# Eight of the mixer's sixteen gate tiles taken out of the recurrence and computed in pairs by seven block products

## The chip, the core and the metric

The kernel runs on one core of one Trainium2 chip. The metric is the device time of one launch in microseconds (us). Five engines work side by side: TensorE (PE in the rows; PEld is its weight load), VectorE (DVE), ScalarE (ACT), GpSimd (POOL) and SyncE (SP), whose queue issues all the transfers spoken of here. Each engine takes its instructions in a fixed order; where one waits, those behind it wait too.

## The reference, cut to what matters

One decoder block over a sequence of 1024 tokens, width 1024: a SwiGLU sublayer, a token mixer, a second SwiGLU sublayer. The change touches two factors of the mixer, the gates g_pool and g_dn, each a product of the normed input with 1024 columns of one weight:

```
proj = h @ mix_w_in
xp, q, k, v, z, b_raw, a_raw, g_pool, g_dn = split(proj)
ya = multiscale_pool(xp) @ pool_w * pool_scale @ pool_proj
o  = gated_delta_rule(q, k, v, ...)          # the recurrence
yb = (rms_norm(o) * silu(z)) @ dn_proj
merged = sigmoid(g_pool) * ya + sigmoid(g_dn) * yb
return merged @ mix_w_out
```

## The kernel before

**Number format.** Every large product is made in three parts: a float32 operand is split into a rounded high part (a cast on ACT, line 134) and the rest (a subtraction on DVE, line 135), and `mm3` (line 165) adds high x high, high x low and low x high. A product of a 128-wide weight tile with one half of the sequence (512 columns) over all 1024 inputs is so 8 x 3 = 24 matmuls of 128x512; a tile of 128 outputs for both halves is 48.

**Stages.** `ffn1`, then the mixer, then `mout` (merge and output projection), then `ffn2`. Both FFN stages use Strassen-Winograd block products (`both`, line 461): a 2 x 2 matrix of weight blocks times a 2 x 2 matrix of blocks of the input takes seven block products of 12 matmuls instead of eight. They need four sums of blocks of the input (`h_sums`, line 376), made once and kept, and sums of weight blocks and of results for each pair, all elementwise on 128x512 tiles.

**The mixer.** It runs 17 units, numbered here from u = 0 to 16. Unit u prepares one half-sequence of one head (`prepare`, line 1087: a chain of 15 steps that alternate between PE and ACT or DVE) and scans the half that unit u - 1 prepared (`scan`, line 1184: four chunks of three steps and an end with a norm and four transposes, line 1233). The last unit, 16, only scans. Into these chains `weave` (line 1354) hands out fill in equal shares: `z`, `q`, `k`, `v` and pool projections and the sixteen gate tiles (`gate_out`, line 1246: 48 matmuls, a sigmoid for each half, a store to `sg_dram`). Odd units 1, 3, 5 and 7 also hold one pool group. The number of gate tiles in a unit is `n`: one in each odd unit from 1 to 13, two in unit 14, four in unit 15, and the three that are left in unit 16.

**Order.** The code is written for a scheduling layer that gives instructions priority by their place in the program, assigns them to engine queues when their inputs are ready by its own model, and reuses memory of a closed pool tile by tile. What it made of the code is a fixed list for each engine.

**After the mixer.** `reload` (line 745) brings back twelve tiles per half (four pooled `p_dram`, eight `y_dram`) through the old x tiles and splits them; `merge` (line 761) multiplies them by the output projections in `ps_t` and `ps_pj` and by the gates read from `sg_dram`. Sums of the conditioning weights `ada_w` (line 201, DVE) run between.

Of the kernel before, what the change touches and what calls it, by code (L numbers as in the profile page):

```python
# [21 lines left out]
NH = T // HALF  # L22
NC = HALF // P
HEADS = 8
# [24 lines left out]
N_MID = 3  # L49
N_OUT = 11  # L50
GROUP = 4
END_PAD = 224
PSUM_OUT = ("inv", "inv", "scan", "oo")

# [12 lines left out]
def block(tc, ctx, xT, vec, cst, invw, ada_w, f1_in, f1_out, f2_in, f2_out, mix_in, mix_ba,  # L67
          pool_w, pool_proj, dn_proj, mix_out, outT):
    nc = tc.nc
# [63 lines left out]
    def split(src, hi, lo, lo_eng=V):  # L133
        S.copy(hi, src)  # L134
        lo_eng.tensor_tensor(out=lo, in0=src, in1=hi.bitcast(F32), op=ALU.subtract)  # L135

    def load(src, t=None):
        t = raw_tile(src.shape[-1]) if t is None else t
        nc.sync.dma_start(t, src)
        return t  # L140
# [205 lines left out]
        return gh, gl  # L346


    def ffn(fpool, x, h, w_in, w_out, gate, done, between=(), first=None):


# [4 lines left out]
        sums = {}  # L356
# [7 lines left out]
        def middle(f, hf, w):  # L364
# [1 line left out]
            mm3(pg, tiles(w[0], KD, h[hf]))  # L366
            mm3(pu, tiles(w[1], KD, h[hf]))
            return swiglu(pg, pu)

        def sub(out, a, b, eng=V):  # L370
            eng.tensor_tensor(out=out, in0=a, in1=b, op=ALU.subtract)  # L371

        def f32(t):
            return t.bitcast(F32)

        def h_sums():

# [67 lines left out]
            early_outs(js, 1)  # L445
            return islice(steps, N_OUT - N_MID)

        def terms(ps, a, b, c, start, stop, chained):

            for n, (u, v) in enumerate(((a[0], b[0]), (a[0], b[1]), (a[1], b[0]))):  # L450
                PE.matmul(ps, lhsT=u[:, c * P:(c + 1) * P], rhs=v, start=start and n == 0,  # L451
                          stop=stop and n == 2, skip_group_check=chained)

        def product(ps, src, hs, start=True):

            w = pair()
            split(src, *w)
            for k in range(4):
                terms(ps, w, hs[k], k, start and k == 0, k == 3, not start)

        def both(f, out, pairs=False):

            (a11, a12), (a21, a22) = [[load(w_in[f, :, i, c * HALF:(c + 1) * HALF])
                                       for c in range(2)] for i in range(2)]
            h11, h21, h22 = h[0][:4], h[0][4:], h[1][4:]
            s1, s2 = nt[:, 0, :], nt[:, 1, :]
# [10 lines left out]
            c11, c12 = bank("pj"), bank("t")  # L477
            product(c11, a11, h11)
            yield
            u = act()  # L480
            S.copy(u, c11)
            V.tensor_tensor(out=s1, in0=a21, in1=a22, op=ALU.add)
            product(c12, s1, sums["1"])
            yield
            v = act()
            S.copy(v, c12)
            sub(s2, s1, a11)
            product(c11, a12, h21, start=False)
            yield
            g0 = act()  # L490
            S.activation(g0, c11, AF.Silu)
            p6 = bank("pj")
            product(p6, s2, sums["2"])
            yield
            V.tensor_tensor(out=u, in0=u, in1=p6, op=ALU.add)
            sub(s2, a12, s2)
            product(c12, s2, h22, start=False)
            yield
            g1 = act()
            V.tensor_tensor(out=g1, in0=u, in1=c12, op=ALU.add)  # L500
            S.activation(g1, g1, AF.Silu)
            p7 = bank("t")
            sub(s1, a11, a21)
            product(p7, s1, sums["3"])
            yield
            V.tensor_tensor(out=u, in0=u, in1=p7, op=ALU.add)
            V.tensor_tensor(out=v, in0=u, in1=v, op=ALU.add)
            p4 = bank("pj")
            product(p4, a22, sums["4"])
            yield  # L510
            V.tensor_tensor(out=u, in0=u, in1=p4, op=ALU.subtract)
            gated_tile(g0, u)
            gated_tile(g1, v)

        def out_group(fs, gs):

# [219 lines left out]
    with phase_pool("mix") as rows, phase_pool("parts") as parts, phase_pool("odds") as odds:  # L736
        wring.set((wpool, 3), (rows, 5))
        mixer(tc, BySize(rows, parts, odds), locals())


    with phase_pool("ffn2") as fpool:
# [68 lines left out]
def mixer(tc, mp, env):  # L810
# [488 lines left out]


    qkv = {0: lead}
    gates = [gate_out(i, m) for m in range(KD) for i in range(2)]
    pools = [pool_group(g) for g in range(4)]
    mixes = []
    zs, preps, states, ds = {}, {}, {}, {}
# [7 lines left out]
    for u in range(HEADS * NH + 1):  # L1313
        hd, hf = divmod(u, NH)
        fill = []
        if hf == 0 and hd < HEADS:
            zs[hd] = []
            fill.append((16, gate_z(hd, zs[hd])))
        if mixes:
            fill.append((2, mixes.pop(0)))  # L1320
        if hf == 0 and hd < HEADS:
            if hd + 1 < HEADS:
                qkv[hd + 1] = [[], [], [], []]
                fill += [(16, conv(4 + j * HEADS + hd + 1, qkv[hd + 1])) for j in range(2)]
            n = 0 if hd + 1 < HEADS else 2
        elif hd + 1 < HEADS:
            fill.append((16, conv(4 + 2 * HEADS + hd + 1, qkv[hd + 1])))
            n = 1
        else:
            n = 4 if hd < HEADS else len(gates)  # L1330
        if pools and hf == 1:
            fill.append((16, pools.pop(0)))
            mixes.append(pool_mix(4 - 1 - len(pools)))
        for _ in range(min(n, len(gates))):
            fill.append((16, gates.pop(0)))
        steps = []
# [115 lines left out]
```

## Time and profile before

| what | value |
| --- | --- |
| time, median of 3 runs | 2526.25 us (2524.32 to 2527.13) |
| the profiled execution's own time | 2523.53 us |
| its span in the trace | 2521.7 us |
| PE busy in the span | 2455.1 us (97%) |
| DVE busy | 1930.0 us (77%) |
| ACT busy | 999.4 us (40%) |
| mixer, start of unit 1 to the last transposes of unit 16 | 829.0 to 1591.6 us |

Matmuls are pipelined: the next one starts before the last ends, so the busy time of PE overstates its work, and what a matmul costs is read from the distance between starts, or from a count over a stretch in which PE never pauses.

### The profile page before, as it was taken

To read this page: it belongs to the slowest core of one execution; us is meant where nothing else is said; L and a number is where in the kernel's file an instruction comes from. 1 tells how busy PE (TensorE), PEld (TensorE's weight loads), DVE (VectorE), ACT (ScalarE), POOL (GpSimd) and SP (SyncE) were. 2 spreads that over 40 slices of the span, in tenths; PEclk is the share of its full clock that TensorE was granted. 3 is DMA by queue.
4 is the path that set the end of the run, shared out by engine and by line. 5 is a ranking of instruction groups with operands and counts; after the bars stand their busy time and mean duration, and the time that the engine had idled before them with its cause. 6 is when DMAs were issued, how large, how long until landed. Compare 5 with 4: busy or idle time off the path is not lost. (4 is left out here: it accounts for less than half of the span.)

```text
span 2521.7 us, 33597 instructions
## 1 busy us (share of the span) xinstructions
PE 2455.1 (97%) x12496; PEld 2000.6 (79%) x12496; DVE 1930.0 (77%) x3300; ACT 999.4 (40%) x1689; POOL 210.9 (8%) x228
## 2 busy tenths in 40 slices
PE   7899999999999999999999999999999999999997
PEld 4678888888767888888888888788777888888875
DVE  6988888888887776867877853767687668788897
ACT  3333333333456444544544542311453233333333
POOL 0500000000030101102000000000241000000003
PEclk9999999999999999999999999999999999999998
DMA  7234322222231112121111122854221122222232
GB/s 271 80 117 137 127 71 68 67 80 80 87 131 43 55 48 73 47 66 58 51 47 42 47 85 88 273 170 159 88 76 46 49 65 84 68 71 71 68 94 77
DMA packets 121556, 222.09 MB, mean 88 GB/s; under 512 B 13616, under 2 KB 14384, under 8 KB 121392
## 3 DMA queue, kind: packets, MB, share of 16 engines
q1 hardware_dynamic: 121392, 219.95, 27.0%
q8 instruction: 98, 1.61, 0.3%
q14 instruction: 66, 0.54, 0.1%
HBM read 194.73 MB, written 25.17 MB: 87 GB/s over the span
## 5 line engine op out<-in xcount | busy, mean ns | idle before, releaser
L134 ACT CAST whi<-raw 128x512 fp32r<-128x512 f32 (+1 forms) x403 | 248.2, 618 | 606.5 <-PE ps_pj L165 155.8
L135 DVE TENSOR_TENSOR wlo<-raw,whi 128x512 fp32r<-128x512 f32 (+1 forms) x403 | 289.1, 722 | 75.3 <-ACT whi L134 73.3
L165 PE MATMUL ps_pj<-hh,whi 128*128 128x512 f32 (+1 forms) x732 | 304.5, 416 | 0.0
L165 PE MATMUL ps_pj<-hh,wlo 128*128 128x512 f32 (+1 forms) x732 | 289.7, 396 | 2.0 <-DVE wlo L135 2.0
L165 PE MATMUL ps_pj<-hl,whi 128*128 128x512 f32 (+1 forms) x732 | 289.5, 396 | 0.0
L134 ACT CAST whi<-nt 128x512 fp32r<-128x512 f32 x160 | 99.5, 622 | 263.3 <-PE ps_pj L451 125.1
L165 PEld LDWEIGHTS ps_pj<-hh,wlo 128*128 128x128 f32 (+1 forms) x732 | 137.1, 187 | 31.2 <-DVE wlo L135 2.5
L135 DVE TENSOR_TENSOR wlo<-nt,whi 128x512 fp32r<-128x512 f32 x160 | 110.1, 688 | 62.6 <-ACT whi L134 62.5
L165 PEld LDWEIGHTS ps_pj<-hh,whi 128*128 128x128 f32 (+1 forms) x732 | 137.5, 188 | 24.2 <-issue 2.9
L165 PEld LDWEIGHTS ps_pj<-hl,whi 128*128 128x128 f32 (+1 forms) x732 | 137.8, 188 | 23.1 <-issue 1.4
L451 PE MATMUL ps_pj<-hh,wlo 128*128 128x512 f32 x320 | 124.8, 390 | 1.0 <-DVE wlo L135 1.0
L451 PE MATMUL ps_pj<-hh,whi 128*128 128x512 f32 x320 | 125.1, 391 | 0.5 <-ACT whi L134 0.5
L451 PE MATMUL ps_pj<-hl,whi 128*128 128x512 f32 x320 | 124.8, 390 | 0.0
L895 DVE SCALAR_TENSOR_TENSOR cacc<-rawseq,vt,cacc 128x512 f32<-128x512 f32 x144 | 107.1, 744 | 0.6
L165 PE MATMUL ps_pj<-hxh,whi 128*128 128x512 f32 (+1 forms) x252 | 103.2, 410 | 0.0
L165 PE MATMUL ps_pj<-hxh,wlo 128*128 128x512 f32 (+1 forms) x252 | 99.0, 394 | 0.4 <-DVE wlo L135 0.4
L165 PE MATMUL ps_pj<-hxl,whi 128*128 128x512 f32 (+1 forms) x252 | 98.8, 393 | 0.0
L226 POOL TENSOR_TENSOR act<-act,nt 128x512 f32<-128x512 f32 x18 | 26.4, 1468 | 807.9 <-ACT nt L233 807.5
L567 DVE SCALAR_TENSOR_TENSOR x<-ps_inv,mod,x 128x512 f32<-128x512 f32 x128 | 89.3, 743 | 0.2
L451 PE MATMUL ps_inv<-opl,whi 128*128 128x512 f32 x224 | 87.7, 392 | 0.0
L451 PE MATMUL ps_inv<-oph,whi 128*128 128x512 f32 x224 | 87.2, 391 | 0.0
L451 PE MATMUL ps_inv<-oph,wlo 128*128 128x512 f32 x224 | 86.8, 389 | 0.0
(477 smaller groups left out, 6367.9 us busy)
## 6 DMA issues: line engine op xcount, KB each, us to landing
raw<-f_in SPq DMA_DIRECT2D x184, 256.0 KB, 3.4
raw<-f_out SPq DMA_DIRECT2D x160, 256.0 KB, 2.8
raw<-ada_w SPq DMA_DIRECT2D x112, 256.0 KB, 3.1
raw<-mix_in SPq DMA_DIRECT2D x104, 256.0 KB, 2.8
ada_raw<-ada_w SPq DMA_DIRECT2D x32, 256.0 KB, 5.3
sg_dram<-sg SPq DMA_DIRECT2D x32, 256.0 KB, 2.0
act<-sg_dram SPq DMA_DIRECT2D x32, 256.0 KB, 3.9
raw<-dn_proj SPq DMA_DIRECT2D x20, 256.0 KB, 3.0
```

The lines of the kernel that those rows point to most:

```text
L134: S.copy(hi, src)
L135: lo_eng.tensor_tensor(out=lo, in0=src, in1=hi.bitcast(F32), op=ALU.subtract)
L165: PE.matmul(ps, lhsT=a, rhs=b, start=n == 0, stop=n == last)
L226: eng.tensor_tensor(out=a, in0=a, in1=b, op=ALU.add)
L451: PE.matmul(ps, lhsT=u[:, c * P:(c + 1) * P], rhs=v, start=start and n == 0, stop=stop and n == 2, skip_group_check=chained)
L567: V.scalar_tensor_tensor(out=x[k][hf], in0=banks[m], scalar=mod[:, gate, k:k + 1], in1=x[k][hf], op0=ALU.mult, op1=ALU.add)
L895: V.scalar_tensor_tensor(out=acc, in0=raw[:, i:i + HALF], scalar=w[:, i:i + 1], in1=acc, op0=ALU.mult, op1=ALU.add)
```

## The change

The generator of the seven products moves out of the FFN into a function `seven` that the FFN and the new code share; the FFN's instructions are the same ones. Of the sixteen gate tiles eight (m = 0 to 3, for both gates) stay in the recurrence: none in units 1, 3, 5 and 7, one each in 9, 11, 13 and 14, two in 15, two in 16. The other eight (m = 4 to 7) form a new stage, `gates`, between the mixer and `mout`: for each m the 2 x 2 matrix of weight blocks has the two gates as rows and the two halves of the 1024 inputs as columns. `gate_sums` makes the four sums of input blocks first, all on DVE and ACT; then four times seven products follow.

```diff
+N_PLAIN = 4
+N_GATE_ACT = 8
...
+    def seven(blocks, h, sums, known):
+        (a11, a12), (a21, a22) = [[load(blocks(i, c)) for c in range(2)] for i in range(2)]
+        h11, h21, h22 = h[0][:4], h[0][4:], h[1][4:]
+        s1, s2 = nt[:, 0, :], nt[:, 1, :]
+        c11, c12 = bank("pj"), bank("t")
+        product(c11, a11, h11)
...
+        S.copy(u, c11)
+        V.tensor_tensor(out=s1, in0=a21, in1=a22, op=ALU.add)
+        product(c12, s1, sums["1"])
...
+        product(c11, a12, h21, start=False)
...
+        known(0, 0, c11)
+        p6 = bank("pj")
+        product(p6, s2, sums["2"])
...
+        product(c12, s2, h22, start=False)
...
+        product(p7, s1, sums["3"])
...
+        product(p4, a22, sums["4"])
+        yield
+        V.tensor_tensor(out=u, in0=u, in1=p4, op=ALU.subtract)
+        known(1, 0, u)
+        known(1, 1, v)
...
+    with phase_pool("gates") as gp:
+        aring.set((gp, N_GATE_ACT))
+        wring.set((wpool, 3))
+        sums = {n: [] for n in "1234"}
+        def gate_sums():
...
+            for k in range(4):
+                b12, t1 = added(h[1][k]), act()
+                less(t1, b12, h[0][k])
+                kept("1", t1)
+                b22 = added(h[1][k + 4])
+                sub(b12, b22, b12)
+                kept("3", b12)
+                sub(b22, b22, t1)
+                kept("2", b22)
+                less(b22, b22, h[0][k + 4])
+                kept("4", b22, h_pair(1, k))
+                yield
...
+        for _ in gate_sums():
+            pass
+        for m in range(N_PLAIN, KD):
+            for _ in gates_of(m):
+                pass
...
-    gates = [gate_out(i, m) for m in range(KD) for i in range(2)]
+    gates = [gate_out(i, m) for m in range(N_PLAIN) for i in range(2)]
...
-            n = 0 if hd + 1 < HEADS else 2
+            n = 0 if hd + 1 < HEADS else 1
...
-            n = 1
+            n = 0 if pools else 1
...
-            n = 4 if hd < HEADS else len(gates)
+            n = 2 if hd < HEADS else len(gates)
```

(`added` is one DVE addition of a high and a low part, `less` two subtractions, `sub` one, `kept` a split, which is one cast on ACT and one subtraction on DVE.)

**DVE, end of the last unit.** Before: L1223 to L1235 are the end of the last scan, L201 the `ada_w` sums, `pl` the first split of the reloaded pool tiles.

```order
L1201 TENSOR_SCALAR vn<-ps_scan,beta 128x128
L201 SCALAR_TENSOR_TENSOR nt<-raw,sc,nt 128x512 x2
L1223 TENSOR_REDUCE so<-sqd 128x4
L1224 SCALAR_TENSOR_TENSOR so<-so,qeps 128x4
L1229 TENSOR_TENSOR x_91<-ps_oo,so 128x512
L201 SCALAR_TENSOR_TENSOR nt<-raw,sc,nt 128x512 x4
L1235 SCALAR_TENSOR_TENSOR x_92<-ps_oo,vt,z 128x512
L201 SCALAR_TENSOR_TENSOR nt<-raw,sc,nt 128x512
L135 TENSOR_TENSOR pl<-x_85,ph 128x512
```

The same place after; L1288 to L1300 are the end of the scan under new line numbers, L770 and L352 the additions and subtractions of `gate_sums`, `t1l` and `t3l` its splits.

```order
L1266 TENSOR_SCALAR vn<-ps_scan,beta 128x128
L1288 TENSOR_REDUCE so<-sqd 128x4
L1289 SCALAR_TENSOR_TENSOR so<-so,qeps 128x4
L1294 TENSOR_TENSOR x_91<-ps_oo,so 128x512
L1300 SCALAR_TENSOR_TENSOR x_92<-ps_oo,vt,z 128x512
L770 TENSOR_TENSOR act<-hxh,hxl 128x512
L352 TENSOR_TENSOR act<-act,hh 128x512
L770 TENSOR_TENSOR act<-hh,hl 128x512
L352 TENSOR_TENSOR act<-act,hl 128x512
L352 TENSOR_TENSOR act<-act 128x512
L770 TENSOR_TENSOR act<-hxh,hxl 128x512
L137 TENSOR_TENSOR t1l<-act,t1h 128x512
```

The whole of `gate_sums` stands behind the last instruction of the last scan, L1300; nothing of it is ahead.

**PE, behind the last transposes** (L1233 before, L1298 after). Before, the merge's products of the reloaded pool tiles `ph` and `pl` come next:

```order
L165 MATMUL ps_pj<-hh,wlo 128x512
L1233 MATMUL ps_oo<-ct,x_91 128x128 x4
L165 MATMUL ps_t<-ph,whi 128x512
L165 MATMUL ps_t<-pl,whi 128x512
L165 MATMUL ps_t<-ph,wlo 128x512
```

After, twelve matmuls on stored input blocks (`hh`, `hl`; the last one is the first row here), then those that read the sums `t1` and `t2`:

```order
L360 MATMUL ps_pj<-hh,wlo 128x512
L360 MATMUL ps_t<-t1h,whi 128x512
L360 MATMUL ps_t<-t1l,whi 128x512
L360 MATMUL ps_t<-t1h,wlo 128x512
L360 MATMUL ps_pj<-t2h,whi 128x512
L360 MATMUL ps_pj<-t2l,whi 128x512
L360 MATMUL ps_t<-t1h,whi 128x512
L360 MATMUL ps_t<-t1l,whi 128x512
L360 MATMUL ps_t<-t1h,wlo 128x512
L360 MATMUL ps_pj<-t2h,wlo 128x512
```

Where reloaded tiles were the first thing PE needed after the scans, it is now sums that DVE begins behind those same scans.

**DVE, from the last gate pair to the first merge, after.** L409 is the last addition of the last pair, L201 and L203 the `ada_w` sums, `pl` the split of the reloaded tiles:

```order
L409 TENSOR_TENSOR act<-act,ps_pj 128x512
L137 TENSOR_TENSOR wlo<-raw,whi 128x512
L201 TENSOR_SCALAR nt<-raw,sc 128x512
L203 SCALAR_TENSOR_TENSOR nt<-raw,sc,nt 128x512
L137 TENSOR_TENSOR pl<-x_85,ph 128x512
```

The merge's first split stood behind the last scan and seven `ada_w` sums; it now stands behind the last result of the gate stage and two.

## Rows read from the trace of the kernel before

**Rows 1.** The page: busy time of PE; granted clock in 40 slices, tenths.

```profile
PE 2455.1 (97%) x12496; PEld 2000.6 (79%) x12496; DVE 1930.0 (77%) x3300; ACT 999.4 (40%) x1689; POOL 210.9 (8%) x228
...
PEclk9999999999999999999999999999999999999998
```

**Rows 2.** Windows, all engines: unit 3 (930.9) and unit 9 (1233.4).

```profile
core 0: us, PE busy (x) PEld busy (x) DVE busy (x) ACT busy (x) POOL busy (x), PEclk, DMA share, GB/s
...
930.90:980.80 49.90, 49.90 (x335) 42.04 (x334) 37.34 (x81) 23.41 (x41) 8.22 (x12) 1.00 0.18 62
...
1233.40:1272.80 39.40, 39.38 (x288) 32.82 (x287) 34.98 (x75) 21.58 (x37) 4.06 (x6) 1.00 0.13 43
```

**Rows 3.** Windows of line 165 alone (PE, PEld): the same units.

```profile
930.90:980.80 49.90, 38.35 (x144) 25.56 (x144) 1.00 0.18 62
...
1233.40:1272.80 39.40, 27.52 (x96) 16.64 (x96) 1.00 0.13 43
```

**Rows 4.** Window of line 451, the FFN's block products (PE, PEld).

```profile
2000.00:2400.00 400.00, 400.00 (x1746) 327.47 (x1745) 1.00 0.23 70
```

**Rows 5.** Timeline of DVE, then ACT: start, us, instruction, count, [idle before].

```profile
1608.95 4.90 DVE L135 TENSOR_TENSOR hl<-x,hh 128x512 fp32r<-128x512 f32 x8
...
1618.59 0.68 DVE L769 TENSOR_TENSOR act<-act,ps_pj 128x512 f32<-128x512 f32 x1
1619.30 0.69 DVE L770 TENSOR_TENSOR act<-act 128x512 f32<-128x512 f32 x1
...
1607.48 4.27 ACT L134 CAST hh<-x 128x512 fp32r<-128x512 f32 x8 [0.29 <-DMA x<-y_dram]
```

**Rows 6.** Unit 16: its window from 1553, and the timeline of its end.

```profile
1553.00:1591.60 38.60, 38.56 (x190) 32.04 (x188) 10.58 (x22) 6.24 (x11) 1.01 (x1) 1.00 0.34 109
...
1583.89 0.39 PE L1208 MATMUL ps_oo<-vn,x 128*128 128x128 f32 x2
1584.31 0.60 ACT L1221 ACTIVATE sqd<-ps_oo 128x512 f32<-128x512 f32 x1 [3.93 <-PE ps_oo L1208]
...
1586.75 1.01 POOL L170 TENSOR_TENSOR so<-so,mhalf 128x4 f32<-128x4 f32 x1 [46.17 <-DVE so L1224]
1587.79 0.69 DVE L1229 TENSOR_TENSOR x<-ps_oo,so 128x512 f32<-128x512 f32 x1 [1.19 <-POOL so L170]
```

**Rows 7.** Timeline: one step of the scan in unit 16, PE then DVE.

```profile
1562.29 0.38 PE L1194 MATMUL ps_scan<-state,x 128*128 128x128 f32 x2
...
1562.71 0.35 DVE L1196 SCALAR_TENSOR_TENSOR r<-ps_scan,neg,v 128x128 f32<-128x128 f32 x1 [3.08 <-PE ps_scan L1194]
```

**Rows 8.** Timeline of PE from the last transposes to the merge.

```profile
1590.96 0.60 PE L1233 MATMUL ps_oo<-ct,x 128*128 128x128 f32 x4
1592.37 0.49 PE L165 MATMUL ps_t<-ph,whi 128*128 128x512 f32 x1 [0.81 <-ACT ph L134]
1597.38 0.79 PE L165 MATMUL ps_t<-pl,whi 128*128 128x512 f32 x1 [4.51 <-DVE pl L135]
...
1598.39 0.63 PE L165 MATMUL ps_t<-ph,whi 128*128 128x512 f32 x1
1598.82 0.63 PE L165 MATMUL ps_t<-pl,whi 128*128 128x512 f32 x1
...
1602.49 0.80 PE L165 MATMUL ps_t<-ph,whi 128*128 128x512 f32 x1 [0.91 <-ACT ph L134]
```

**Rows 9.** Windows of the same place, all engines, with the granted clock.

```profile
1591.60:1597.40 5.80, 0.52 (x2) 0.21 (x2) 3.60 (x6) 3.83 (x8) 0.00 (x0) 0.88 0.76 240
1597.40:1606.20 8.80, 7.89 (x18) 5.72 (x19) 6.72 (x11) 2.18 (x4) 0.00 (x0) 0.50 0.91 306
```

**Rows 10.** Timeline of DVE, then ACT, at the same place.

```profile
1595.97 0.75 DVE L201 SCALAR_TENSOR_TENSOR nt<-raw,sc,nt 128x512 f32<-128x512 f32 x1 [1.01 <-DMA raw<-ada_w]
1596.64 1.89 DVE L135 TENSOR_TENSOR pl<-x,ph 128x512 fp32r<-128x512 f32 x3
...
1601.82 2.18 ACT L134 CAST ph<-x 128x512 fp32r<-128x512 f32 x4 [6.39 <-DMA x<-p_dram]
```

More of the change, by code (lines that the diff above doesn't have):

```diff
@@ L346, in gated, with sub, f32, terms @@
         return gh, gl
+    def sub(out, a, b, eng=V):
+        eng.tensor_tensor(out=out, in0=a, in1=b, op=ALU.subtract)
+    def f32(t):
+        return t.bitcast(F32)
+    def terms(ps, a, b, c, start, stop, chained):
+        for n, (u, v) in enumerate(((a[0], b[0]), (a[0], b[1]), (a[1], b[0]))):
+            PE.matmul(ps, lhsT=u[:, c * P:(c + 1) * P], rhs=v, start=start and n == 0,
+                      stop=stop and n == 2, skip_group_check=chained)
+    def product(ps, src, hs, start=True):
+        w = pair()
+        split(src, *w)
+        for k in range(4):
+            terms(ps, w, hs[k], k, start and k == 0, k == 3, not start)
+    def seven(blocks, h, sums, known):
[5 more added lines that the diff above has]
+        yield
+        u = act()
+        S.copy(u, c11)
+        V.tensor_tensor(out=s1, in0=a21, in1=a22, op=ALU.add)
+        product(c12, s1, sums["1"])
+        yield
+        v = act()
+        S.copy(v, c12)
+        sub(s2, s1, a11)
+        product(c11, a12, h21, start=False)
+        yield
+        known(0, 0, c11)
+        p6 = bank("pj")
+        product(p6, s2, sums["2"])
+        yield
+        V.tensor_tensor(out=u, in0=u, in1=p6, op=ALU.add)
+        sub(s2, a12, s2)
+        product(c12, s2, h22, start=False)
+        yield
+        g1 = act()
+        V.tensor_tensor(out=g1, in0=u, in1=c12, op=ALU.add)
+        known(0, 1, g1)
+        p7 = bank("t")
+        sub(s1, a11, a21)
+        product(p7, s1, sums["3"])
+        yield
+        V.tensor_tensor(out=u, in0=u, in1=p7, op=ALU.add)
+        V.tensor_tensor(out=v, in0=u, in1=v, op=ALU.add)
+        p4 = bank("pj")
+        product(p4, a22, sums["4"])
+        yield
+        V.tensor_tensor(out=u, in0=u, in1=p4, op=ALU.subtract)
+        known(1, 0, u)
+        known(1, 1, v)
     def ffn(fpool, x, h, w_in, w_out, gate, done, between=(), first=None):
@@ L368, in middle @@
             return swiglu(pg, pu)
[L370 to L374, printed above, removed]
         def h_sums():
@@ L446, in lead @@
             return islice(steps, N_OUT - N_MID)
[L448 to L459, printed above, removed]
         def both(f, out, pairs=False):
[L463 to L466, printed above, removed]
             def gated_tile(a, b):
@@ L475, in gated_tile, with known @@
                 out.append(t)
[L477 to L513, printed above, removed]
+            gate = {}
+            def known(i, hf, t):
+                if i:
+                    gated_tile(gate[hf], t)
+                    return
+                gate[hf] = act() if hf == 0 else t
+                S.activation(gate[hf], t, AF.Silu)
+            yield from seven(lambda i, c: w_in[f, :, i, c * HALF:(c + 1) * HALF], h, sums, known)
         def out_group(fs, gs):
@@ L738, in block, with kept, added, less @@
         mixer(tc, BySize(rows, parts, odds), locals())
+    with phase_pool("gates") as gp:
[3 more added lines that the diff above has]
+        def gate_sums():
+            def kept(n, src, p=None):
+                p = p or tuple(gp.tile([P, HALF], F32R, tag=f"t{n}{e}", name=f"t{n}{e}", bufs=4)
+                               for e in "hl")
+                split(src, *p)
+                sums[n].append(p)
+            def added(p):
+                t = act()
+                V.tensor_tensor(out=t, in0=f32(p[0]), in1=f32(p[1]), op=ALU.add)
+                return t
+            def less(t, a, p):
+                sub(t, a, f32(p[0]))
+                sub(t, t, f32(p[1]))
+            for k in range(4):
+                b12, t1 = added(h[1][k]), act()
[8 more added lines that the diff above has]
+                kept("4", b22, h_pair(1, k))
+                yield
+        def gates_of(m):
+            def known(i, hf, t):
+                out = act() if (i, hf) == (0, 0) else t
+                S.activation(out, t, AF.Sigmoid)
+                nc.sync.dma_start(sg_dram[i, m, hf], out)
+            return seven(lambda i, c: mix_in[36 + i * KD + m, :, c * HALF:(c + 1) * HALF],
+                         h, sums, known)
+        for _ in gate_sums():
[3 more added lines that the diff above has]
+                pass
     with phase_pool("ffn2") as fpool:
```

## The prediction

> **What bounds the kernel now.** I read the page first. PE is busy for 97% of the span and its granted clock is full in nearly every slice [rows 1], so the question is what PE does in the stages that the change touches, and where it would stop. The windows of single units answer the first part. Unit 3, with 144 large matmuls, lasts 49.9 us; unit 9, with 96, lasts 39.4 us [rows 2, 3]. The difference, 10.5 us for 48 matmuls, is 0.219 us each, close to what one costs where PE never pauses: 400 us for 1746 of the block products, 0.229 us [rows 4]. So the recurrence's chains are hidden behind the fill even at 96, and PE bounds the mixer. The timeline around the last scan answers the second part. After the transposes of unit 16 PE stops for 0.81, 4.51 and 0.91 us [rows 8], first for a cast, then for a split that DVE makes late [rows 10], then for the next transfer; and the clock falls to half, 1.2 GHz, in the 8.8 us that follow [rows 9], with 0.43 us from one matmul to the next [rows 8]. This seam is the one place in the mixer where PE really waits. The change puts a new stage into it.
>
> **Part 1: matmuls saved.** Eight plain tiles of 48 matmuls go, 384. Four pairs of seven products of 12 come, 336. That is 48 fewer, at 0.229 us [rows 4]: **-11.0 us**. It is all that the change can save on PE, and a pair's 84 matmuls are 19.2 us of work.
>
> **Part 2: less cover in the units.** Units 1, 3, 5 and 7 go from 144 to 96 large matmuls, 14 loses 48, 15 and 16 lose 144 together. Between units 3 and 9 that step gave back 10.5 us where the matmuls alone are 11.0, so each tile taken out leaves 0.5 us of stalls. Unlike unit 9, units 1 to 7 hold a pool group: DVE is busy for 37.3 us in unit 3 [rows 2], and 36.1 us remain when the gate tile's two splits (0.60 us each) leave, in a unit of 39.4 us; I add 0.3 us for each of the four. For unit 16 I looked at the scan: from a step's first matmul (1562.29) to the end of DVE's answer (1563.06) is 0.8 us [rows 7]; the cover per step falls from nine matmuls (2.1 us) to six (1.4 us) and still suffices. At the unit's end the norm takes from 1583.89 to 1588.48, 4.6 us [rows 6], with 18 matmuls (4.1 us) to cover it: 0.5 us. Together 7 x 0.5 + 4 x 0.3 = **+4.7 us**. Bounds: 2 us, if the difference of 3 and 9 is mostly the pool group's own work, and 9 us, if units 1 to 7 stall for 1.5 us each.
>
> **Part 3: the sums of input blocks.** This is the large term. DVE's list after the change holds nothing of `gate_sums` ahead of the end of the last scan, and PE's list holds only 12 matmuls that need no sum before those that do. So for the first pair PE runs at DVE's pace. I count from the start of L1300, the last scan's result, which is also about when PE passes its transposes. DVE issues a 128x512 subtraction every 0.60 us (8 in 4.90 us), or 0.71 us behind one whose result it reads [rows 5]; ACT casts one in 0.52 us [rows 5]. In DVE's list the splits of sum 1 (k = 0 to 3) stand at places 7, 17, 29 and 41 behind L1300, those of sum 2 at 12, 23, 36 and 47, the last one of sum 4 at 53 and the weights of the last product at 54. Place 41 is over at 0.7 + 41 x 0.602 = 25.4 us. The other half of the first output block (12 matmuls without a sum) can't fill in: on ACT the copy of that bank stands behind the cast of the fourth sum 1, at 24 us. By then PE has been able to run 31 of the 84 matmuls.
>
> From there I followed the lists by hand. If PE had full clock: those 12 and the two of the last sum 1 end at 27.8 us; ACT copies the second bank (27.4) and only then casts the fourth sum 2 (28.0); DVE splits it (29.1); three matmuls (29.7); DVE adds the result and splits the three remaining weight tiles by 33.9 us; the last 30 matmuls run from 32.2 to 39.1 us. PE will not have full clock: with 31 matmuls in 24 us it waits far more than in the seam of before, where waits of 0.8 and 4.5 us were enough for the lower level [rows 8, 9]. At 0.43 us each [rows 8] until about 33 us, the same steps end at 41.3 us. I take 40.7 us, nearer to the half clock that the rows show. Less the pair's own 19.2 us this is **+21.5 us** of waiting. Bounds: 19.5 us (full clock throughout) and 25 us (five more of the chained subtractions and casts in line, or the low clock up to the end). Pairs two to four have their sums ready and run as the FFN's do [rows 4]: nothing.
>
> The Trainium skill ("TensorE: Matmul & The Clock Gate", HAM oscillation) tells the same of another kernel, in which PE ran short bursts between waits and started each one throttled, and advises to restructure so that the work is contiguous. It speaks against a stage that opens with 24 us of bursts; without any such effect my sum would be 1.6 us lower, and the seam of before agrees with the rule, half clock behind the wait [rows 9].
>
> **Part 4: the seam to the merge.** Before, PE passes from the transposes (1591.56) to its second merge matmul at 1597.38, 5.8 us, and then works 8.8 us at half clock, which costs 18 x 0.2 = 3.6 us, and 0.9 us more for a transfer [rows 8, 9]: some 10 us. Does the new stage hide that? The reloads could come back early, but the first split of a reloaded tile (`pl`) stands on DVE behind the last addition of the last gate pair, a weight split and two `ada_w` sums, the second of which waits for a transfer into a buffer that this weight split frees. From the last matmul: 0.4 us for its result, 0.69 for the addition, 0.6 for the split, about 3 us for the transfer (the row of before waited 1.01 us in a like place [rows 10]), 0.75 for the sum, 0.6 for `pl`: about 6 us against 5.8. The fourth pool tile still reuses the first one's place and returns some 4 us later, as the cast that waits 6.39 us shows [rows 10]. So the seam moves behind the gates nearly whole: **+0.5 us**. Bounds: -8 us if the transfer is early and the clock holds, +3 us.
>
> **The sum.** -11.0 + 4.7 + 21.5 + 0.5 = **+15.7 us**. The profiled execution took 2523.5 us, so it would take 2539.2 us. The median of the runs shown, 2526.25 us, is 2.7 us above that execution; +15.7 us on it is 2541.9, and I say **2541 us**, slower. About 0.2%, 5 us, is what a measurement of this kernel can tell from no change.
>
> **The rivals.**
>
> A. Faster: the sums are hidden. In the last 38.6 us of unit 16 DVE works 10.6 us [rows 6]; the 28 us that it idles would hold nearly all of 53 x 0.60 = 32 us of sums, and the first pair would cover the rest. Then part 3 is zero and the sum is -11.0 + 4.7 + 0.5 = -5.8 us, 2520 us. Each us that the first sum starts before L1300 takes one us off part 3, and the sign turns at about 16 us. Against it stands the fixed list: L1300 is ahead of every sum on DVE. Only a misread list would bring this about: chance 0.04. The Trainium skill's rule in "Perfetto Trace Analysis" (Identifying the Most-Contended Engine), that the engine with the highest occupancy is the one to relieve first, would go still further: counting PE's work alone gives -11.0 us, 2515 us. The rows bear it out inside the units [rows 2 to 4], not at the seam, where PE waits [rows 8].
>
> B. The seam vanishes. The reloaded tiles are back, the raw buffers are early, and PE goes hot into the merge: part 4 is -8 us, the sum +7.2 us, 2533 us. For it: most `y_dram` transfers move ahead into the mixer's end, and five `ada_w` sums fewer stand before `pl`. Against it: `pl` is still behind a result of the last matmul and a transfer. Chance 0.13.
>
> C. The units with pool groups run into DVE (36 of 39 us, with GpSimd at work beside it), and the sums are at their long bound: parts 2 and 3 at 9 and 25, the sum +23.5 us, 2549 us. Chance 0.11.
>
> That the change doesn't do what it says can be left out: the lists show 48 matmuls fewer and the new stage.
>
> **How the numbers follow.** The forecast (2534 to 2547 us, parts 2 to 4 a few us about their values) has 0.72, B 0.13, C 0.11, A 0.04. The range reaches over B's lower side and to C: low 2531 us (-11 + 3 + 19.5 - 6.5 = +5), high 2550 us. Slower by over 0.2% (above 2531.3) are the forecast, C, and some three quarters of B: 0.92 and a little caution, 0.90; within 0.2% the rest of B and part of A: 0.06; faster 0.04.
>
> **What would show it.** In the profile after, windows of units 3, 5 and 7 of 39.5 to 40.5 us each (below 39: part 2 is wrong; above 41: C). Between the last transposes and the first matmul of the second pair about 41 us, with PE idle or at half clock for half of it, waiting for DVE `t1l` and `t2l`; if this stretch is under 30 us, part 3 is wrong and with it the sign. Three further pairs of 19 to 20 us each; if they are longer, something I took as free isn't. From the last product to the second merge matmul 5 to 7 us and then a stretch at half clock; if PE goes on within 2 us, B. The prediction as a whole fails if the first sum's additions run before the last scan step.

## The result, and the profile after

The kernel after takes 2548.97 us (median; 2547.04 to 2550.26) beside 2526.69 us for the kernel before on the same chip: ratio 1.0093, 95% interval 1.0081 to 1.0104. It is slower, as forecast, by 22.3 us where 14.8 us (2541 against 2526.25) were forecast. The profiled execution has a span of 2545.3 us, 23.6 us above that of before. Of its page, the rows that answer to [rows 1]: 48 matmuls fewer, 96 DVE instructions more, and a slice of the clock row, behind the middle, that is no longer full.

```profile
PE 2459.4 (97%) x12448; PEld 1992.7 (78%) x12448; DVE 1989.5 (78%) x3396; ACT 1010.9 (40%) x1718; POOL 210.8 (8%) x228
...
PEclk9999999999999999999999998999999999999998
```

**The units.** Windows of units 3, 5, 7, 8 and 9, with the columns of [rows 2]:

```profile
920.90:961.60 40.70, 40.00 (x288) 32.58 (x287) 36.41 (x78) 20.41 (x36) 6.60 (x10) 1.00 0.09 29
1012.20:1057.20 45.00, 42.57 (x287) 34.92 (x286) 36.73 (x78) 20.72 (x37) 7.62 (x11) 0.93 0.12 37
1108.20:1151.30 43.10, 39.86 (x288) 32.72 (x287) 36.15 (x77) 20.36 (x36) 8.91 (x12) 1.00 0.10 31
1151.30:1204.30 53.00, 51.04 (x335) 42.72 (x334) 36.65 (x74) 23.60 (x41) 6.80 (x11) 1.00 0.21 68
1204.30:1243.70 39.40, 39.38 (x287) 32.81 (x287) 34.94 (x75) 21.57 (x37) 4.05 (x6) 1.00 0.13 43
```

Unit 9, which the change leaves alone, is as long as before [rows 2]. Units 3, 5 and 7 have the same number of large matmuls as unit 9 now, and are 1.3, 5.6 and 3.7 us longer than it. The granted clock is 0.93 of full in unit 5.

**The new stage and the seam.** Windows of the four pairs, and of the 9.1 us behind the last product:

```profile
1518.73:1558.15 39.42, 28.64 (x88) 17.47 (x86) 38.17 (x63) 16.09 (x28) 0.00 (x0) 0.74 0.19 61
1558.15:1577.19 19.04, 19.04 (x86) 15.77 (x84) 10.94 (x17) 8.06 (x14) 0.00 (x0) 1.00 0.33 111
1577.19:1596.23 19.04, 19.04 (x86) 15.77 (x84) 10.52 (x16) 7.70 (x14) 0.00 (x0) 1.00 0.33 110
1596.23:1615.04 18.81, 18.81 (x84) 15.58 (x83) 8.53 (x13) 7.46 (x14) 0.00 (x0) 1.00 0.40 126
1615.04:1624.16 9.12, 3.84 (x10) 2.56 (x9) 6.13 (x11) 5.12 (x10) 0.00 (x0) 0.81 0.71 227
```

In the first pair DVE is busy for 38.2 of 39.4 us and PE runs at a mean clock of 0.74; the others are pure PE work.

Put together from the starts of PE's instructions (first `prepare` of unit 0, last transposes, last product, last matmul of the program):

| stretch | before, us | after, us | difference | of it matmuls | the rest |
| --- | --- | --- | --- | --- | --- |
| up to unit 0 | 795.6 | 794.9 | -0.7 | 0 | -0.7 |
| units 0 to 16 | 795.7 | 723.8 | -71.9 | 384 x 0.229 = -87.9 | +16.0 |
| gate stage | 0 | 96.3 | +96.3 | 336 x 0.229 = +76.9 | +19.4 |
| last product (before: last transposes) to the end of PE | 921.2 | 921.0 | -0.2 | 0 | -0.2 |

The matmuls give back 11.0 us, as in part 1; the units lose 16.0 us of that, not 4.7; the stage loses 19.4 us; the seam nothing.

Beside the experiments below the kernel before took 2524.60 to 2525.30 us, 1.4 to 2.1 us less than beside the kernel after. A difference in time between an experiment and the kernel after is uncertain by about that much; stretches are compared within the traces.

### The profile page after: what moved, and what is told of

It reads as the page before. It is cut to its first block, busy times and chain, and to the rows that moved or that the text cites. A ratio compares the mean times of both kernels' runs of the same rounds, so it can differ in the third digit from the quotient of the medians.

```text
span 2545.3 us, 33687 instructions
## 1 busy us (share of the span) xinstructions
PE 2459.4 (97%) x12448; PEld 1992.7 (78%) x12448; DVE 1989.5 (78%) x3396; ACT 1010.9 (40%) x1718; POOL 210.8 (8%) x228
## 5 line engine op out<-in xcount | busy, mean ns | idle before, releaser
L167 PE MATMUL ps_pj<-hh,whi 128*128 128x512 f32 (+1 forms) x636 | 267.6, 421 | 0.0
L167 PE MATMUL ps_pj<-hh,wlo 128*128 128x512 f32 (+1 forms) x636 | 253.9, 399 | 2.1 <-DVE wlo L137 2.1
L167 PE MATMUL ps_pj<-hl,whi 128*128 128x512 f32 (+1 forms) x636 | 254.0, 399 | 0.0
L167 PEld LDWEIGHTS ps_pj<-hh,wlo 128*128 128x128 f32 (+1 forms) x636 | 119.6, 188 | 26.7 <-DVE wlo L137 2.5
L360 PE MATMUL ps_pj<-hh,whi 128*128 128x512 f32 x352 | 138.2, 393 | 0.5 <-ACT whi L136 0.5
L360 PE MATMUL ps_pj<-hh,wlo 128*128 128x512 f32 x352 | 137.6, 391 | 1.0 <-DVE wlo L137 1.0
L360 PE MATMUL ps_pj<-hl,whi 128*128 128x512 f32 x352 | 137.7, 391 | 0.0
L167 PEld LDWEIGHTS ps_pj<-hl,whi 128*128 128x128 f32 (+1 forms) x636 | 120.3, 189 | 19.9 <-issue 1.9
L167 PEld LDWEIGHTS ps_pj<-hh,whi 128*128 128x128 f32 (+1 forms) x636 | 120.0, 189 | 20.2 <-issue 2.2
L167 PE MATMUL ps_pj<-hxh,whi 128*128 128x512 f32 (+1 forms) x220 | 90.6, 413 | 0.0
L360 PE MATMUL ps_inv<-oph,wlo 128*128 128x512 f32 x224 | 86.8, 389 | 0.0
```

The costliest lines, as they stand in the source:

```text
L167: PE.matmul(ps, lhsT=a, rhs=b, start=n == 0, stop=n == last)
```

## Experiments: where the 16 us in the units are

By pairs of units, counted between transposes and less the matmuls taken out, units 3 and 4 lose 1.7 us, 5 and 6 lose 6.5, 7 and 8 lose 5.8, and 9 to 12 nothing. The pool groups of units 1, 3, 5 and 7 make one, two, three and four window sums for each half.

**Theory A.** Without a gate tile behind them the pool group's products are the last fill of units 1, 3, 5 and 7. Their results come when the scan's norm does, and the window sums on GpSimd and the DVE subtraction that reads them stand ahead of this norm in two queues. **Theory B**, that of the prediction's rival C: DVE as a whole is too busy. In unit 5 of the kernel before, GpSimd has made the window sums 0.9 us before it is handed the norm's factors `so`:

```profile
1069.69 2.26 POOL L1271 TENSOR_TENSOR wsum<-wsum 128x525 f32<-128x525 f32 x2
1072.83 1.40 POOL L170 TENSOR_TENSOR so<-so,mhalf 128x4 f32<-128x4 f32 x1 [0.88 <-DVE so L1224]
```

The rows of unit 5 of the kernel after, timeline of GpSimd, then DVE, then PE:

```profile
1046.17 1.54 POOL L1336 TENSOR_TENSOR wsum<-wsum 128x525 f32<-128x525 f32 x1
1047.67 1.01 POOL L172 TENSOR_TENSOR so<-so,mhalf 128x4 f32<-128x4 f32 x1
1048.67 1.05 POOL L1336 TENSOR_TENSOR wsum<-wsum 128x521 f32<-128x521 f32 x1
...
1046.71 0.68 DVE L1235 TENSOR_TENSOR er<-ps_inv,y 128x512 fp32r<-128x512 f32 x1
1049.75 0.69 DVE L1340 SCALAR_TENSOR_TENSOR x<-wsum,praw 128x512 f32<-128x512 f32 x1 [2.36 <-POOL wsum L1336]
1050.36 0.17 DVE L1344 TENSOR_TENSOR pfix<-wsum,invt 128x16 f32<-128x16 f32 x1
1050.44 0.68 DVE L1294 TENSOR_TENSOR x<-ps_oo,so 128x512 f32<-128x512 f32 x1
...
1048.63 0.39 PE L167 MATMUL ps_pj<-hh,wlo 128*128 128x512 f32 x1
1051.18 1.11 PE L1298 MATMUL ps_oo<-ct,x 128*128 128x128 f32 x4 [2.16 <-DVE x L1294]
```

Read them from the bottom. PE waits 2.16 us for L1294, the scan's normed output. L1294 needs `so`, which GpSimd has made by 1048.68, but on DVE it stands behind L1340, which waits 2.36 us for the last window sum; and `so` itself stood on GpSimd behind a window sum of 1.54 us. DVE idles meanwhile: it isn't full, it is held. In unit 7 of the same trace L1294 stands ahead of L1340 and waits for `so` alone; there PE stops twice, for 1.69 us before the transposes and for 1.52 us before a product whose operand stands on DVE behind L1340. Behind the stop in unit 5 the clock is at half for 6.8 us (1050.72 to 1057.55).

**The spread alone.** All sixteen tiles plain, four in unit 15 and eight in 16, no new stage, so that the matmuls are those of before and only the spread in units 0 to 14 is that of after:

```diff
-N_PLAIN = 4
+N_PLAIN = 8
...
-            n = 2 if hd < HEADS else len(gates)
+            n = 4 if hd < HEADS else len(gates)
```

> The spread alone: all sixteen gate tiles stay plain and the new stage is gone, but units 0 to 14 hold the gate tiles that the changed kernel gives them (none in 1, 3, 5, 7); the four more that are left then run in unit 15 and eight in unit 16. Theory 1 (the units of the recurrence lose some 16 us when the gate tile leaves units 1 to 7, which the trace of the changed kernel shows as units 0 to 8 saving only 31 of the 44 us of matmuls taken out): 2526.7 + 13 to 16 = 2540 to 2543 us, unit 5 at 45 us and unit 7 at 43 us. Theory 2 (as forecast, 0.5 to 0.8 us per tile, and what the trace showed in units 5 and 7 comes with something else of the new stage): 2530 us.

Measured: 2539.36 us, ratio 1.0054 (1.0041 to 1.0066), 14 us above before with not a matmul changed; units 0 to 16 take 810.4 us, 14.7 more than before. The time is just below theory 1's 2540 to 2543 us. Units 5 and 7 (windows):

```profile
1012.70:1055.00 42.30, 39.90 (x287) 32.47 (x286) 36.23 (x78) 20.29 (x36) 7.62 (x11) 1.00 0.08 27
...
1106.40:1149.50 43.10, 39.86 (x288) 32.72 (x287) 36.15 (x77) 20.37 (x36) 8.93 (x12) 1.00 0.10 31
```

So the loss is the spread's own. Unit 5 is 2.7 us shorter than in the kernel after, and not at the 45 us expected: here the clock stays full through it.

**Without the window sums.** GpSimd's additions are left out, so the pooled values are others; all else stands.

```diff
-            for i in range(g + 1):
+            for i in range(0):
```

> The changed kernel with the window sums of the pool groups left out (the loop of GpSimd additions runs zero times, so the pooled values are others): GpSimd is then almost idle in units 1 to 8 and DVE's subtraction waits for nothing. Theory A: units 5 and 7 at 39.5 to 40.5 us, as unit 9, the time down by 9 to 13 us, 2536 to 2540 us. Theory B (DVE's load): DVE keeps all but the time that GpSimd's additions cost it, units 5 and 7 above 42 us, the time down by 4 us at most.

Measured: 2537.64 us, 1.0050 (1.0038 to 1.0063), 11.3 us below the kernel after. Units 0 to 16 take 711.7 us, 12.1 less. The same units:

```profile
1013.80:1053.10 39.30, 39.28 (x287) 32.72 (x286) 34.51 (x76) 20.43 (x36) 4.30 (x8) 1.00 0.09 29
...
1104.60:1144.00 39.40, 39.38 (x287) 32.81 (x287) 35.85 (x78) 20.51 (x36) 4.29 (x8) 1.00 0.12 37
```

DVE is as busy in unit 7 as in the kernel after (35.85 against 36.15 us), and PE no longer stops: theory B falls. What is left over the matmuls, 3.9 us, is about what part 2 had given the whole (4.7 us).

**Pool group first.** The same work, with the pool group's products ahead of the convolution's in these four units:

```diff
+        mixed = bool(mixes)
...
-            fill.append((16, pools.pop(0)))
+            fill.insert(1 if mixed else 0, (16, pools.pop(0)))
```

> The changed kernel with one line moved: in units 1, 3, 5 and 7 the pool group's products stand ahead of the convolution's in the fill, so that GpSimd's window sums and DVE's subtraction of them end well before the scan's norm. Theory A (in units 5 and 7 the norm's instructions on GpSimd and DVE stand behind the pool group's, and the transposes wait): units 5 and 7 fall from 45.0 and 43.1 us to about 40, their successors give back 2, the half clock of 6.8 us in unit 5 goes, together 8 to 11 us, 2538 to 2541 us. Theory B (DVE is too full for units of 96 matmuls): no change, 2547 to 2551 us.

Measured: 2545.00 us, 1.0077 (1.0063 to 1.0091). Units 0 to 16 take 716.2 us, 7.6 less than after: units 3, 5 and 7 are 40.0, 39.7 and 41.6 us. In unit 5 (timeline of GpSimd) the window sums are over at 1041.3, and the norm's `so` has nothing ahead of it:

```profile
1039.10 2.19 POOL L1336 TENSOR_TENSOR wsum<-wsum 128x525 f32<-128x525 f32 x2
...
1047.43 1.01 POOL L172 TENSOR_TENSOR so<-so,mhalf 128x4 f32<-128x4 f32 x1
```

So it is the place of the sums, not their amount, that costs nearly two thirds of the 12 us. The total fell by only 4.0 us where 8 to 11 were expected (1.9 us between the spans of the two traces): 3.8 us were lost behind the gate stage. The clock was at half there from 1612.15 to 1618.98 and from 1673.59 to 1677.00, 10.2 us, where the kernel after has 3.4 us of it; the extra 6.8 us at half clock are 3.4 us of work. Why the clock fell there is open.

## Experiments: the stage and the seam

**No sums.** Stored blocks of the input in place of the sums (the values of eight gate tiles are others):

```diff
-        for _ in gate_sums():
-            pass
+        for k in range(4):
+            for n, p in (("1", h[0][k]), ("2", h[0][k + 4]), ("3", h[1][k + 4]), ("4", h[1][k])):
+                sums[n].append(p)
```

> The changed kernel without the sums of input blocks: the products read input blocks that are there already in the place of the four sums, so the eight gate tiles of the new stage are left with other values; the rest of the work is the same. If PE waits there for DVE's 53 instructions, the first pair falls from 39.4 to about 19.2 us and the time by about 20 us, to 2529 us. If the wait belongs to the start of a stage as such (the clock, weights that load late), the first pair stays above 30 us and the time above 2540 us.

Measured: 2519.14 us, 0.9975 (0.9966 to 0.9984), 29.8 us below the kernel after. The first pair is pure PE work like the others (window), and the stage takes 76.1 us:

```profile
1519.80:1538.98 19.18, 19.18 (x88) 15.85 (x86) 12.94 (x21) 10.49 (x19) 0.00 (x0) 1.00 0.69 220
```

That is the 20 us of part 3. The other 10 are not. 6.6 us came behind the last product (914.4 us to the end of PE in place of 921.0), where the merge followed at once; the last 3 can't be placed in the traces, whose spans differ by only 25.9 us. PE at the seam, first in this kernel, then in the kernel after:

```profile
1595.87 0.39 PE L360 MATMUL ps_pj<-hxh,wlo 128*128 128x512 f32 x1
1596.10 0.39 PE L167 MATMUL ps_t<-ph,whi 128*128 128x512 f32 x1
1596.32 0.39 PE L167 MATMUL ps_t<-pl,whi 128*128 128x512 f32 x1
```

```profile
1615.04 0.39 PE L360 MATMUL ps_pj<-hxh,wlo 128*128 128x512 f32 x1
1617.38 0.50 PE L167 MATMUL ps_t<-ph,whi 128*128 128x512 f32 x1 [1.95 <-ACT ph L136]
1621.21 0.79 PE L167 MATMUL ps_t<-pl,whi 128*128 128x512 f32 x1 [3.33 <-DVE pl L137]
```

DVE there, in the kernel after: the last addition of the stage, the `ada_w` sum that waits for its transfer, and `pl`:

```profile
1615.47 0.69 DVE L409 TENSOR_TENSOR act<-act,ps_pj 128x512 f32<-128x512 f32 x1 [0.83 <-PE ps_pj L360]
...
1619.80 0.75 DVE L203 SCALAR_TENSOR_TENSOR nt<-raw,sc,nt 128x512 f32<-128x512 f32 x1 [2.51 <-DMA raw<-ada_w]
1620.47 1.89 DVE L137 TENSOR_TENSOR pl<-x,ph 128x512 fp32r<-128x512 f32 x3
```

**Kept sums in pools of their own.** Why did that wait go? My guess from the order of the pools: without sums, the 24 tiles of sums 1 to 3 lie free when the merge's first staging tiles want that memory. Here the sums stay and only their place changes, so that these tiles lie over sums that are read early:

```diff
-    with phase_pool("gates") as gp:
+    with phase_pool("gates") as gp, phase_pool("g3") as g3, phase_pool("g1") as g1, \
+            phase_pool("g2") as g2:
+        held = {"1": g1, "2": g2, "3": g3}
...
-                p = p or tuple(gp.tile([P, HALF], F32R, tag=f"t{n}{e}", name=f"t{n}{e}", bufs=4)
+                p = p or tuple(held[n].tile([P, HALF], F32R, tag=f"t{n}{e}", name=f"t{n}{e}", bufs=4)
```

> Asks whether the seam to the merge hangs on memory: only the place of the sums' tiles changes. The kernel after, with the kept sums 1, 2 and 3 in pools of their own, so that the merge's first staging tiles lie over sums whose last reader is an early product of the last pair and not over the whole pool of the stage; in DVE's list the first split of a reloaded tile stands at the same place as in the run without sums, ahead of the last addition. Theory (the staging tile waits for the last reader of the memory under it): from the last product to the end of PE's work 914 to 916 us in place of 921, first matmul of the merge within 1 us of the last product; pairs still 39.4 and 19 us: 2541 to 2544 us. Rival (in the run without sums the seam went because DVE and the clock were undisturbed before it, memory has no part): 921 us from the last product to the end, 2549 us.

Measured: 2544.30 us, 1.0072 (1.0060 to 1.0085). The first pair takes 39.5 us as before, and the merge follows at once (PE):

```profile
1615.03 0.39 PE L360 MATMUL ps_pj<-hxh,wlo 128*128 128x512 f32 x1
1615.25 0.39 PE L167 MATMUL ps_t<-ph,whi 128*128 128x512 f32 x1
```

So memory made the seam's wait: with nothing changed but the place of the sums, the first `pl` stands ahead of the last addition of the stage on DVE (1608.50 and 1615.75). That its tile had lain over memory that the stage still read fits this; no address was read out. But from the last product to the end of PE it is 917.9 us, not the 914 to 916 expected: 3.1 of the 6.6 us came back. The trace shows where PE waits instead, 22 us further on, for a product with a stored gate (L835) whose transfer is late (PE, then DVE):

```profile
1637.63 0.60 PE L167 MATMUL ps_t<-ph,whi 128*128 128x512 f32 x1 [4.75 <-DVE act L835]
...
1636.88 0.69 DVE L835 TENSOR_TENSOR act<-act,ps_t 128x512 f32<-128x512 f32 x1 [4.83 <-DMA act<-sg_dram]
```

3.4 us at half clock follow. In the kernel without sums DVE waits 4.65 us at the like place, and PE doesn't stop there for more than 0.3 us. So most of the wait moved and did not vanish. The kernels below that have these pools and the blocks ahead also go on at once; they stop for 3.6 to 4.8 us some 11 us behind the last product, for a cast of the next reloaded tiles, and take 918.7 to 920.5 us to the end of PE.

**First output blocks ahead.** If part 3 is only a matter of order, the 96 matmuls of the four first output blocks, which need no sums, can cover the sums: 22 us of products ahead. The kept sums lie in pools of their own here too, and the ring of tiles `act` has twelve in place of eight.

```diff
+        ahead = [first_block(m) for m in range(N_PLAIN, KD)]
+        for g0, g1_ in zip(ahead[::2], ahead[1::2]):
+            for _ in zip(g0, g1_):
+                pass
+        gate_sums()
+        for m in range(N_PLAIN, KD):
+            six(m)
```

(`first_block` is the two products of one block and its sigmoid, `six` the other five products of a pair; `gate_sums` makes all four parts of sum 1 first, then 2, 3, 4.)

> Asks whether the 20 us of the first pair are only the order of the work: the same 336 matmuls, but the 96 of the first output block of all four pairs, which need no sum of input blocks, run first (22 us), and the sums are made in the order in which the products want them, all four of sum 1, then 2, 3, 4. Theory (PE waits for DVE's sums because only 12 matmuls stand ahead of them): the whole stage falls from 96.3 us to 78 to 84 us, at full clock, and the seam shortens as in the kernel with the sums in pools of their own: 2527 to 2534 us. Rival (DVE's and ACT's total work for sums, weights and copies bounds the stage whatever the order): the stage stays above 90 us and the time above 2540 us.

Measured: 2550.79 us, 1.0097 (1.0084 to 1.0111), and the stage takes 101.3 us: a miss by 20. The window of the first 84 matmuls is pure work, that of the next 84 is not; and DVE's timeline, below it, shows its first addition of a sum (L789) 20.8 us behind the last scan's result (L1345):

```profile
1518.57:1537.72 19.15, 19.15 (x87) 15.85 (x86) 6.89 (x10) 7.19 (x14) 0.00 (x0) 1.00 0.50 165
1537.72:1582.06 44.34, 31.48 (x85) 19.32 (x84) 40.00 (x65) 17.05 (x29) 0.00 (x0) 0.69 0.18 61
```

```profile
1518.85 0.75 DVE L1345 SCALAR_TENSOR_TENSOR x<-ps_oo,vt,z 128x512 f32<-128x512 f32 x1 [1.15 <-PE ps_oo L1343]
...
1539.68 0.68 DVE L789 TENSOR_TENSOR act<-hxh,hxl 128x512 f32<-128x512 f32 x1
```

DVE is busy for 6.9 of the first 19.2 us and makes no sum in them. The results of the blocks ahead and the terms of the sums take their tiles from one ring, in the order of the program, so no sum could have a tile before the last block ahead had one. The scheduling layer wrote that into DVE's list; the next run tests it. This kernel with the pool group first took 2544.53 us (1.0072, 1.0059 to 1.0086): 6.3 us less, where 7 were expected, but with the stage at 101.7 us far from the 2517 to 2525 us that had been expected of both together.

**The same with tiles of their own**, one line:

```diff
-            out = act() if (i, hf) == (0, 0) else t
+            out = up.tile([P, HALF], F32, tag="o", name="o", bufs=4) if (i, hf) == (0, 0) else t
```

> One line against the kernel with the first output blocks ahead (which took 101.3 us from the last transposes to the last product): the results of the four blocks ahead lie in tiles of their own instead of the ring from which the sums take theirs. There the sums' additions stood on DVE behind the whole stretch ahead; now, by the lists, they stand between its weight splits, the last split of sum 1 at place 23 behind the last scan's result and of sum 2 at place 39. Theory (PE waited for the place of the sums in DVE's list, not for their work): place 39 is over 24 us behind the last scan, when PE has 22 us of products without sums behind it, so the stage takes 78 to 84 us, at full clock: 18 to 22 us less than the kernel with the blocks ahead, 2529 to 2533 us. Rival (the engines' work for sums, weights and copies bounds the stage): above 90 us, above 2540 us.

Measured: 2538.07 us, 1.0056 (1.0043 to 1.0069), 12.7 us less; the stage takes 89.5 us, not 78 to 84. So the shared ring cost 11.8 us of the stage. The sums ran beside the products, but PE still stopped once, and DVE's timeline shows for what: the first sum of weight blocks (`nt`, L818) stands behind nearly all the sums of input blocks.

```profile
1540.99 0.39 PE L360 MATMUL ps_pj<-hh,wlo 128*128 128x512 f32 x1
1552.06 0.79 PE L360 MATMUL ps_t<-t1h,whi 128*128 128x512 f32 x1 [10.68 <-ACT whi L136]
...
1550.61 0.69 DVE L818 TENSOR_TENSOR nt<-raw 128x512 f32<-128x512 f32 x1
```

I had counted the places of the splits of the sums, and not that of the weights that meet them.

**Sums in the recurrence.** DVE's idle time in the last units is where rival A put the sums. In the kernel after they can't go there by the order of the pools, since theirs is opened when the recurrence's is closed. But in unit 16 tiles of `prepare` are dead, and they are views of the x tiles. So the unsplit sums 1 and 2 (20 of the instructions) are made there, and 3 and 4 are derived from sum 2:

```diff
+    raw1, raw2 = [*x[0], *x[1]], [*x[2], x[5][0], x[7][0]]
+    for k in range(4):
+        for t, p in ((raw1[k], h[1][k]), (raw2[k], h[1][k + 4])):
+            V.tensor_tensor(out=t, in0=f32(p[0]), in1=f32(p[1]), op=ALU.add)
+        less(raw1[k], raw1[k], h[0][k])
+        sub(raw2[k], raw2[k], raw1[k])
...
+            for k in range(4):
+                kept("1", raw1[k])
+            for k in range(4):
+                kept("2", raw2[k])
+            for n, k0 in (("3", 0), ("4", 4)):
+                for k in range(4):
+                    t = act()
+                    less(t, raw2[k], h[0][k0 + k])
+                    kept(n, t, h_pair(1, k) if k0 else None)
```

> One thing moved in the kernel after: the unsplit sums 1 and 2 of the input blocks (20 of the 53 DVE instructions ahead of the last of them) are made during units 15 and 16, in x tiles that the recurrence no longer uses; the splits, and sums 3 and 4 derived from sum 2, stay where they were. The seven products keep their order. Theory (the 20 us before the second pair are DVE's list behind the last scan): the last of sum 2 is split at place 10 behind the last scan's result instead of 47 and the last of sum 4 at place 33 instead of 53, so the first pair takes 22 to 26 us instead of 39.4 and the time falls by 13 to 17 us, to 2532 to 2536 us; units 15 and 16 stay within 2 us of 62.1. Rival (the first pair waits for something that was covered by the sums: ACT's casts, the block loads, the memory of the new stage): the pair stays above 32 us, the time above 2541 us.

Measured: 2541.37 us, 1.0070 (1.0056 to 1.0084), 7.6 us below the kernel after where 13 to 17 were expected. Units 15 and 16 take 62.1 us as in the kernel after, with 9.6 us more of DVE's work in them: rival A's premise holds, once there is memory. The first pair takes 33.2 us, which is the rival in the expectation (above 32 us, and above 2541 us). It runs without a pause for 5.8 us, and then (PE, and below it ACT):

```profile
1524.43 0.39 PE L360 MATMUL ps_pj<-t2l,whi 128*128 128x512 f32 x1
1535.91 0.79 PE L360 MATMUL ps_pj<-hh,whi 128*128 128x512 f32 x1 [11.09 <-ACT act L380]
...
1534.75 0.62 ACT L136 CAST hxh<-act 128x512 fp32r<-128x512 f32 x1 [1.79 <-DVE act L352]
1535.28 0.58 ACT L380 COPY act<-ps_pj 128x512 f32<-128x512 f32 x1
```

A copy that was ready at 1521.6 stands on ACT behind the casts of sums 3 and 4, which wait for DVE. It was the same in the kernel after, where this copy starts at 1542.71, hidden under the other waits.

**Early sums, blocks ahead and pools together**, and then with the pool group first (edits as above):

> The early sums and, with them, the first output block of all four pairs ahead of the products that need a sum, and the kept sums in pools of their own. Theory: nothing is left for PE to wait for, the stage from the last transposes to the last product takes 77 to 80 us instead of 96.3, at full clock, and the merge follows at once as in the kernel with the pools of their own: 2526 to 2531 us. Rival (as in the kernel with the blocks ahead and the sums late, a wait that DVE's list makes somewhere keeps the stage above 85 us): above 2536 us.

> The same with the pool group's products ahead of the convolution's in units 1, 3, 5 and 7. Theory (the three losses add up and each has its own cause): 6 to 8 us less than without, 2519 to 2524 us, a little under the kernel before (2525). Rival (they don't add): above 2526 us.

Measured: 2538.75 us (1.0057, 1.0044 to 1.0070) and 2530.61 us (1.0022, 1.0013 to 1.0031). The stage takes 88.2 and 86.8 us, so the first one missed; the second is 8.1 us below the first, 6 to 8 expected, but not under the kernel before. The sums 3 and 4 still shared the ring.

**The same with tiles of their own** for the blocks ahead (the one line above):

> The same one line in the kernel with everything together (raw sums made in units 15 and 16, first blocks ahead, kept sums in pools of their own, pool group's products first), which took 2530.6 us with 86.9 us from the last transposes to the last product. By the lists the last split of sum 3 moves from behind the blocks ahead to place 28 behind the last scan, that of sum 4 to 39. Theory: nothing waits for a sum any more, the stage takes 77 to 81 us, the time 2520 to 2526 us, the kernel before's within its uncertainty. Rival (the 10 us beyond the work have another cause): no change, 2529 us or more.

Measured: 2522.03 us, 0.9992 (0.9983 to 1.0001): the kernel before's time within the uncertainty, 27 us below the kernel after. The stage takes 78.6 us, for 76.9 of work; windows of its first two quarters (the other two are pure PE work, 19.0 and 18.8 us):

```profile
1511.20:1530.35 19.15, 19.15 (x87) 15.86 (x86) 18.82 (x32) 13.47 (x25) 0.00 (x0) 1.00 0.75 243
1530.35:1551.90 21.55, 19.61 (x85) 15.62 (x84) 17.74 (x29) 9.90 (x17) 0.00 (x0) 1.00 0.51 161
```

DVE has 18.8 us of work in the first quarter and PE never waits for it. So the 20 us of part 3 were order and memory, not work: part of the sums is made in units 15 and 16 here, where DVE had idled.

## Why the prediction was right in sign and short in size

- **Part 1** (-11.0 us): right. The later pairs take 19.04 us, and 84 x 0.229 is 19.2.
- **Part 2** (+4.7 us, bounds 2 to 9): this is the step that failed; it measured +16.0. The sentence at fault is that on DVE's 36 us in a unit of 39.4, with "0.3 us for each of the four". It reads a share of busy time, and asks whether DVE has room. What decides is where in the unit the pool group's results come and what stands behind their consumer on DVE and GpSimd. The lists showed that the gate tile had been the last fill of these units; I didn't ask what is last now. Rival C named the right units with the wrong mechanism (a full DVE), and too low a price, 9 us; by the prediction's own sign (above 41 us: C) units 5 and 7 pointed to it. Of the 16 us, 12.1 go with the window sums. The 3.9 that are left are near the 3.5 us of the seven times 0.5 us, but no wait was traced for them; units 15 and 16, to which I had given the scan's end, lost 0.5 us in all (94.6 to 62.1 us for three tiles, 33.0 us).
- **Part 3** (+21.5 us): right. The first pair took 39.4 us (forecast 40.7), 20.2 above its work, DVE was busy for 38.2 us of it, and the clock was at half from 1525.17 to 1545.65, until 27 us behind L1300 and not 33. Its use of the Trainium skill ("TensorE: Matmul & The Clock Gate", HAM oscillation) stands: the bursts ran at the lower level.
- **Part 4** (+0.5 us): right in size, -0.2 measured. The second merge matmul came 6.2 us behind the last product (5 to 7 forecast), through the chain given: the last addition, a weight split, an `ada_w` sum that waited 2.51 us for its transfer, `pl`. The half clock behind it lasted 3.4 us, not 8.8. I had not seen that the place of the sums in memory had set this order.
- **The rivals.** B (the seam vanishes) did not come. With the sums elsewhere the wait at the seam goes, but 3.1 us came of it, not 8. A did not come for the reason given, the fixed list; its premise was sound.
- **The sum** was +15.7 us and is +23.6 us by the spans: of the 7.9 us between, part 2 is +11.3, part 3 -2.1, part 4 -0.7, and the start of the mixer -0.7. 2548.97 us lies at the upper end of the range (2531 to 2550 us), and that is luck: this end is rival C's, with 9 us for part 2 and 25 us for part 3, where 16.0 and 19.4 us were measured.

## What to carry to other kernels

When work is taken out of a stage as cover, look for what becomes the last piece of the stage, and for what stands behind its consumers on the in-order engines; an engine's busy share can't show that. When work is put in front of an engine that waits, ask of each of its inputs, the small ones too, at which place of which list it is made; two repairs here missed because one tile ring or one copy tied the lists together. A stage's memory decides whether its preparation can start early: compare addresses, not only dependences. And look for the next wait behind the one that was taken away: at the seam most of it came back 11 to 22 us later.

## What was unexpected of the hardware

The same stop did not always cost the clock. In unit 5 PE stops for 2.15 to 2.17 us before the transposes in eight of these kernels. In two of them (the kernel after, and the one with sums in the recurrence) 6.8 us at half clock follow, and in the kernel after the unit takes 45.0 us. In the other six (the spread alone, no sums, pools of their own, both with blocks ahead, and early sums with blocks ahead) the clock stays full there, and the unit takes 42.3 us with the spread alone; it falls for 3.4 us in unit 8 instead (with the spread alone from 1160.09 to 1163.51), behind stops of 1.0 and 0.9 us. In units 7 and 8 of the kernel after, with stops of 1.69 and 1.52 us and then of 1.1 and 0.9 us, the clock stays full. What decides is open. As 6.8 us at half clock are 3.4 us of work, my estimate is that a forecast of such short stops has to carry about 3 us for each as an uncertainty.
